# A chain of two transformer blocks on one core: the list scheduler's clock with a read port shared by VectorE and GpSimd, and the additions of the norms on VectorE

## The chip, the cores and the metric

The kernel runs on one core of one Trainium2 chip. The metric is the device time of one execution in microseconds (us); the median of three runs before the change is 2174.5 us (2173.39 to 2176.55). Engines are called PE (TensorE, matrix multiplication), DVE (VectorE), ACT (ScalarE), POOL (GpSimd) and SP (SyncE, here an issuer of DMAs).

## The reference

The input is one sequence of 512 tokens of width 1024, all in float32. Two chains of layers follow each other. Cut to its steps:

```
# first block
f = swiglu(rms_norm(h, g_ffn1_pre), gate, up, down);  h = h + 0.5 * rms_norm(f, g_ffn1_post)
u = rms_norm(h, g_mix_pre);  qkv = u @ w_in           # 8 heads of each of two attentions
o_a = stick_breaking_attention(...);  o_b = chunk_band_attention(...)
h = h + rms_norm(concat(rms_norm(o_a), rms_norm(o_b)) @ w_out, g_mix_post)
f = swiglu(rms_norm(h, g_ffn2_pre), ...);             h = h + 0.5 * rms_norm(f, g_ffn2_post)
e = (p @ w_ple_proj) * sigmoid(h @ w_ple_gate);       h = h + rms_norm(e, g_ple_post)
# second block, each: x = x + mixer(rms_norm_2(x, norm_w[i]))
conv_mixer      # gated causal convolution, 3 taps
fox_mixer       # softmax attention with a forget gate, 8 heads of 128
gdn_mixer       # gated delta rule in chunks, 8 heads of 128
swa_mixer       # sliding window attention with sinks, rotary positions
return rms_norm_2(x, final_norm_w)
```

rms_norm(x, g) is x * rsqrt(mean(x*x) + eps) * g over the 1024 channels of a token.

## The kernel before

**Layout.** Activations lie transposed: channels on the 128 partitions, the 512 tokens along the free axis, so the residual stream is eight tiles h[0..7] of 128x512. Weights come from HBM in chunks of 128x512 through four staging tiles wst. Each chunk, and each activation that enters a matrix multiplication, is split into a rounded high part (ACT copies to fp32r) and a remainder (DVE subtracts), and every product is three matmuls: high by high, low by high, high by low (`gemm`, `gemm_two`, `vproj`).

**Norms.** A norm is a sum over channels. `Norm.add` squares a tile on ACT and adds the square to an accumulator; the first tile is written straight to it. With `later` the addition is made on POOL (`G1`), else on DVE. `Norm.stats` turns the accumulator into means with matmuls that are one column wide (`L682`, ps<-cst,t 128x1) and takes the inverse root, on DVE and ACT with `soon`, else by 13 small operations of which 12 are on POOL (`rsqrt`). `Norm.rows` spreads the result over the partitions by transposes (`L687`). There are two kinds of joints between layers:

- `post_norm` (after ffn1, the mixing, ffn2 and the gated projection): the output f is normed and added to h, in two halves of 256 tokens. For each half and each of eight tiles: t = f * gain * r (DVE, one input in PSUM), h = h + t (POOL for the five tiles of `ON_POOL`, DVE for three), the high part (ACT), the square (ACT), its addition (POOL, where another norm follows, which is so at three of the four), and the remainder (DVE).
- `residual_gemm` (after conv, fox and gdn): each output tile is added to h from PSUM (DVE), split, squared, and the square is added on POOL, in 128x512.

**What sets the order.** The program is written out by a list scheduler that runs while the kernel is traced. `Eng.__getattr__` gives each operation of ACT, DVE, POOL and SP a cost in ns and queues it as an `Op`; `free` holds the time at which each engine is free, `at` and `used` when each part of a tile was written and last used, `LAG` the delay from one engine to another. `next_op` picks the operation that can start first, and among those within 20 ns of it the one of lowest priority number (`V0` and `A0` have -1, `V`, `A` and `G` 0, `V1`, `A1` and `G1` 1; weight splits -2 where they are needed soon, else 1). PE is written by the main sequence of matmuls; after each product `poll` lets tasks (attention heads, norms) take a turn when their inputs were ready 150 ns before PE's clock (`MARGIN`). `thin` keeps short matmuls from following each other for long. `mm` and `transpose` price PE's instructions. Each engine then works through its instructions in the order written; semaphores keep the data right, so a price that is wrong makes an engine wait, and nothing else.

```
AHEAD = 300.0
MARGIN = 150.0
POOL = {"affine_select": (127, 0.91), "memset": (36, 0.83), "tensor_scalar": (160, 1.0), "tensor_copy": (120, 3.3)}
```

Nearly all operations of ACT, DVE, POOL and SP are issued at one line of a helper, L391, so rows are told apart by tiles: h is the residual stream, wst a weight chunk, ps a PSUM bank, t any 128x512 work tile, b and a small ones.

Of the kernel before, what the change touches and what calls it, by code (L numbers as in the profile page):

```python
# [12 lines left out]
ALU = mybir.AluOpType  # L13
# [188 lines left out]
def chain_kernel(ctx, tc, xT, pT, wall, params, consts, chbias, pos, out):  # L202
# [83 lines left out]

    class Op:


        def __init__(self, key, run, outs, ins, cost, prio=0, func=None, more=0):  # L290
            self.key, self.run, self.outs, self.ins, self.cost, self.more = key, run, outs, ins, cost, more
            self.prio, self.func = prio, func
            self.deps, self.next = set(), []
            for x, w in [(x, True) for x in outs] + [(x, False) for x in ins]:
                for o in conflicts(x, w):
                    if o not in self.deps:
                        self.deps.add(o)
                        o.next.append(self)
            for x, w in [(x, True) for x in outs] + [(x, False) for x in ins]:
                live.setdefault(name(x), []).append((self, parts(x)[0], w))  # L300
            pending[key].append(self)
# [10 lines left out]
        def start(self):  # L312
            return max([free[self.key]] + [there(x, self.key) for x in self.ins] + [unused(x, self.key) for x in self.outs])

        def trace(self):
            for o in list(self.deps):
                o.trace()
            t = self.start() + self.cost
            k = self.load()
            if k is not None:  # L320
                table[0] = k
                t += 1280
            self.run()
            free[self.key] = t
            pending[self.key].remove(self)
            for x in self.outs + self.ins:
                live[name(x)] = [e for e in live[name(x)] if e[0] is not self]
            key, t = (self.key, t) if not self.more else ("SP", t + self.more)
            for x in self.ins:
                touch(x, t, key)  # L330
            for x in self.outs:
                touch(x, t, key, True)
            for o in self.next:
                o.deps.discard(self)

    def next_op():

        best, when = None, NEVER
        for ops in pending.values():
            can = [(o.start(), o) for o in ops if not o.deps]  # L340
            if can:
                t0 = min(c[0] for c in can)
                t, o = min((c for c in can if c[0] <= t0 + 20), key=lambda c: c[1].rank())
                if t < when:
                    best, when = o, t
        return best, when
# [11 lines left out]
    class Eng:  # L358
# [6 lines left out]
        def __getattr__(self, op):  # L365
            f = getattr(self.eng, op)

            def call(*a, **kw):
# [22 lines left out]
                Op(self.key, lambda: f(*a, **kw), outs, ins, cost, self.prio, func, more)  # L391
# [276 lines left out]

    def mm(ps, lhsT, rhs, start=True, stop=True, tile=None, **kw):
        ps, lhsT, rhs = raw(ps), raw(lhsT), raw(rhs)  # L670
        n = max(parts(rhs)[1], 64)
        if tile is not None:
            ns = tile
        elif rhs.dtype == F32:
            ns = 4 * n / 2.4 + 2.5
        elif rhs.dtype == F32R:
            ns = (n if n >= 256 else 4 * n) / 2.4 + 2.5
        else:
            ns = n / 2.4
        thin[0] = max(0.0, thin[0] + (ns if tile is not None else -0.5 * ns))  # L680
        product(ps, (lhsT, rhs), ns)
        PE.matmul(ps, lhsT, rhs, start=start, stop=stop, **kw)  # L682

    def transpose(ps, src, idn):
        ps, src, idn = raw(ps), raw(src), raw(idn)
        product(ps, (src, idn), 107.0)
        PE.transpose(ps, src, idn)  # L687
# [110 lines left out]
    class Norm:  # L798
# [8 lines left out]
        def add(self, src, cols, later=False):  # L807
# [7 lines left out]
            else:  # L815
                sq = T("sq")
                a.activation(sq[:, c], src, AF.Square)
                (G1 if later else V0).tensor_tensor(self.acc[:, c], self.acc[:, c], sq[:, c], ALU.add)

        def stats(self, cols, soon=False):  # L820
# [3 lines left out]
            for j in range(c0 // P, c1 // P):  # L824
                mm(pc[:, j : j + 1], self.acc[:, j * P : j * P + P], meanc[:, self.mcol : self.mcol + 1], start=j == c0 // P,
                   skip_group_check=True, tile=187)
# [82 lines left out]
    def post_norm(pn, f, gain, nxt_gain, with_norm):  # L909
# [3 lines left out]
        def go(cols):  # L913
            c = slice(*cols)

            def g():
# [5 lines left out]
                for k in range(9):  # L922
                    if k < 8:
                        t = T("pt")
                        V.scalar_tensor_tensor(t[:, c], f[k][:, c], gain[:, k : k + 1], rb, ALU.mult, ALU.mult)
                        (G if k in ON_POOL else V).tensor_tensor(h[k][:, c], h[k][:, c], t[:, c], ALU.add)
# [173 lines left out]
    def soft_heads(heads, span, done, own, causal=False, ready=lambda: True):  # L1100
# [46 lines left out]
        def weigh(qt):  # L1147
            k0, n = span(qt)
            for j in range(n // P):
                for i, (rows, qk, bias, values, sinks) in enumerate(heads):  # L1150
                    mm(po[rows, qt * P : qt * P + P], values(k0 // P + j), ptb[qt, i][:, j * P : j * P + P],
                       start=j == 0, stop=j == n // P - 1, skip_group_check=True, tile=134 if len(heads) > 1 else None)
# [24 lines left out]
    def mixing(S1):  # L1177
# [45 lines left out]
        def sb_pair(p):  # L1223
# [93 lines left out]
            for kt in range(4):  # L1317
                for e in range(2):
                    hd = 2 * p + e
                    mm(po[rows[e], kt * P :], va[kt][:, hd * 64 : hd * 64 + 64], at_(a[place[kt, e][0]], kt, e), start=kt == 0, stop=kt == 3, skip_group_check=True,  # L1320
                       tile=0.95 * (S - kt * P))
# [285 lines left out]
    def gdn_layer(S1):  # L1607
# [18 lines left out]
        def gates(t):  # L1626
            yield t[0:64]
            pt = PS("bat")
            for c in range(4):
                mm(pt[:, c * 16 : c * 16 + 16], t[0:64, c * P : c * P + P], con("ident32")[0:64, 0:16], tile=187)  # L1630
# [60 lines left out]
        def head(hd):  # L1691
# [88 lines left out]
            def mm32(ps, lhsT, rhs):  # L1780
                for c in range(4):
                    for g in range(4):
                        gs, cs = slice(32 * g, 32 * g + 32), slice(32 * c, 32 * c + 32)
                        mm(ps[gs, cs], lhsT[gs, cs], rhs[gs, cs], tile=34)
# [27 lines left out]
            for c in range(4):  # L1812
                cs = slice(32 * c, 32 * c + 32)
                for a, b in zip(lo, hi):
                    mm(p5[b, cs], nL[a, c * P + b.start : c * P + b.stop], Tm[a, cs], tile=34)
# [8 lines left out]
            for c in range(4):  # L1824
                cs = slice(32 * c, 32 * c + 32)
                mm(p7[hi[0], cs], U[hi[0], cs], M5[hi[0], cs], tile=34)
                for a, b in zip(lo, hi):
                    mm(p6[a, cs], M5[b, cs], U[b, cs], tile=34)
# [6 lines left out]
            for c in range(4):  # L1835
                cs = slice(64 * c, 64 * c + 64)
                mm(p8[64:P, cs], nL[0:64, c * P + 64 : c * P + P], T64[0:64, cs], tile=50)
# [302 lines left out]
```

## Time and profile before

| what | value |
|---|---|
| median of three runs | 2174.5 us |
| profiled execution, its own time | 2176.79 us |
| its span, first to last instruction | 2175.1 us |
| PE busy | 2116.3 us, 97% |
| DVE, ACT, POOL busy | 1324.4, 999.2, 299.5 us |
| mean granted clock of PE | 0.99 |

The own time of the profiled execution is 1.7 us more than its span. Times in rows are us from the span's start unless they say ns. In a timeline row the first number is the start, the second the length, xN how many instructions are merged, and the bracket holds the idle time before and what ended it. Consecutive instructions of one engine overlap a little, so a group's busy time can be more than the stretch it fills.

### The profile page before, as it was taken

What the parts mean: (1) busy time and instruction counts of PE and PEld (TensorE: products, weight loads), DVE (VectorE), ACT (ScalarE), POOL (GpSimd) and SP (SyncE); (2) the same over time, 40 slices, a digit from 0 to 9 for tenths busy, and PEclk for the clock granted to TensorE, in tenths of its full rate; (3) what the DMA queues carried; (4) which work ended last, traced back from release to release, by engine and by line L of the source; (5) the groups of instructions that cost most, each with busy time, mean ns of one, the idle gap of its engine ahead of it and who ended that gap; (6) DMA issues with size and microseconds to landing.
All of it is one profiled execution on the core that took longest, in us unless ns stands there. A gap on an engine that the chain in (4) does not pass through costs nothing.

```text
span 2175.1 us, 35809 instructions
## 1 busy us (share of the span) xinstructions
PE 2116.3 (97%) x13583; PEld 1778.1 (82%) x13583; DVE 1324.4 (61%) x2783; ACT 999.2 (46%) x2187; POOL 299.5 (14%) x600
## 2 busy tenths in 40 slices
PE   8999999999999999999999999999998999999998
PEld 7888889988779888889988887888877877778777
DVE  5433455787867442455785554266568677665896
ACT  5332333676855332333642234344446554533764
POOL 0000001311113000000120012000015242221320
PEclk9999999999999999999999999999999999999999
DMA  5232241222221332232223333312222222222221
GB/s 170 97 97 93 96 139 56 69 70 81 64 88 52 105 112 83 97 115 71 92 73 97 97 97 115 116 59 68 69 85 70 60 55 59 61 83 86 85 83 59
DMA packets 105404, 186.11 MB, mean 86 GB/s; under 512 B 12392, under 2 KB 18952, under 8 KB 105232
## 3 DMA queue, kind: packets, MB, share of 16 engines
q1 hardware_dynamic: 103920, 179.62, 26.6%
q0 software_dynamic: 1312, 4.21, 0.6%
q8 instruction: 106, 1.74, 0.3%
q14 instruction: 66, 0.54, 0.1%
HBM read 179.03 MB, written 2.13 MB: 83 GB/s over the span
## 4 chain that ended last, share of the span: by engine, by line
PE 82%; DVE 11%; POOL 3%; ACT 2%; issue 2%; DMA 1%; SPq 0%; DVEq 0%; POOLq 0%; ACTq 0%
PE ps L682 80%; DVE t L391 9%; ACT t L391 2%; PE ps L687 2%; POOL b L391 2%; DVE h L391 1%; POOL t L391 1%; DVE b L391 0%; DMA wst<-in_wall_dram 0%; DMA h<-in_xT_dram 0%; ACT L391 0%; DVE pad L391 0%; SPq L391 0%; POOL h L391 0%; DVE a L391 0%
## 5 line engine op out<-in xcount | busy, mean ns | idle before, releaser
L682 PE MATMUL ps<-t,t 128*128 128x512 f32 (+4 forms) x10648 | 2035.2, 353 | 22.1 <-ACT t L391 11.3
L682 PEld LDWEIGHTS ps<-t,t 128*128 128x128 f32 (+2 forms) x10648 | 1678.2, 186 | 320.7 <-issue 24.4
L391 DVE TENSOR_TENSOR t<-wst,t 128x512 fp32r<-128x512 f32 (+1 forms) x646 | 448.4, 719 | 252.6 <-ACT t L391 250.7
L391 ACT ACTIVATE t<-t 128x512 f32<-128x512 f32 (+4 forms) x470 | 260.3, 569 | 608.8 <-DVE t L391 602.0
L391 ACT ACTIVATE t<-wst 128x512 fp32r<-128x512 f32 (+1 forms) x646 | 380.8, 621 | 98.3 <-DMA wst<-in_wall_dram 94.9
L391 DVE TENSOR_TENSOR t<-ps,t 128x512 f32<-128x512 f32 (+2 forms) x247 | 156.1, 638 | 297.7 <-PE ps L682 296.0
L391 DVE TENSOR_TENSOR t<-t,t 128x512 fp32r<-128x512 f32 (+6 forms) x387 | 238.4, 631 | 66.7 <-ACT t L391 60.8
L391 ACT ACTIVATE t<-ps 128x512 f32<-128x512 f32 (+5 forms) x357 | 140.5, 418 | 239.0 <-PE ps L682 155.5
L391 POOL TENSOR_TENSOR t<-t,t 128x512 f32<-128x512 f32 (+1 forms) x99 | 120.0, 1213 | 542.1 <-ACT t L391 463.7
L391 POOL TENSOR_TENSOR h<-h,t 128x256 f32<-128x256 f32 x40 | 34.7, 874 | 795.5 <-DVE t L391 793.9
L391 ACT ACTIVATE t<-t,a 128x257 f32<-128x257 f32 (+5 forms) x128 | 66.2, 518 | 49.4 <-DVE a L391 46.8
L391 ACT ACTIVATE t<-h,prm 128x256 fp32r<-128x256 f32 (+1 forms) x80 | 46.4, 588 | 83.4 <-DVE h L391 69.8
L391 DVE SCALAR_TENSOR_TENSOR t<-h,prm,t 128x256 fp32r<-128x256 f32 (+1 forms) x80 | 64.2, 815 | 9.0 <-ACT t L391 9.0
L391 DVE SCALAR_TENSOR_TENSOR t<-pad,prm,t 128x512 f32<-128x512 f32 (+1 forms) x92 | 68.7, 755 | 0.8
L687 PE MATMUL ps<-cst,t 128*128 128x128 f32 x400 | 63.1, 279 | 2.5 <-DVE t L391 1.7
L391 ACT ACT_TABLE_LOAD x48 | 61.6, 1283 | 5.7 <-DVE a L391 4.1
L687 PEld LDWEIGHTS ps<-cst,t 128*128 128x128 f32 x400 | 48.6, 143 | 14.8 <-DVE t L391 2.5
L391 ACT ACTIVATE t<-h 128x256 f32<-128x256 f32 (+2 forms) x112 | 49.6, 466 | 22.6 <-DVE h L391 20.3
L391 POOL TENSOR_SCALAR b<-b 128x4 f32<-128x4 f32 (+3 forms) x84 | 26.1, 310 | 206.8 <-DVE b L391 201.7
L682 PEld LDWEIGHTS ps<-t 32*32 32x32 f32 (+1 forms) x2304 | 33.1, 109 | 24.3 <-DVE t L391 10.4
L391 DVE TENSOR_SCALAR t<-t,a 128x256 f32<-128x256 f32 (+3 forms) x128 | 49.2, 394 | 2.3
L391 POOL TENSOR_SCALAR_AFFINE_SELECT t<-t 128x256 f32<-128x256 f32 (+2 forms) x48 | 27.3, 571 | 168.0 <-DVE t L391 117.1
(93 smaller groups left out, 693.1 us busy)
## 6 DMA issues: line engine op xcount, KB each, us to landing
wst<-in_wall_dram SPq DMA_DIRECT2D x644, 256.0 KB, 2.7
t<-t SPq DMA_DIRECT2D x40, 64.0 KB, 2.0
h<-in_xT_dram SPq DMA_DIRECT2D x8, 256.0 KB, 5.3
t<-in_chbias_dram POOLq DMA_DIRECT2D x8, 256.0 KB, 3.7
t<-cdr POOLq DMA_DIRECT2D x8, 256.0 KB, 6.4
t<-gdr SPq DMA_DIRECT2D x32, 64.0 KB, 3.7
out_dram<-t SPq DMA_DIRECT2D x16, 128.0 KB, 1.8
cst<-in_consts_dram SPq DMA_DIRECT2D x1, 626.0 KB, 6.3
```

The costliest lines, as they stand in the source:

```text
L391: Op(self.key, lambda: f(*a, **kw), outs, ins, cost, self.prio, func, more)
L682: PE.matmul(ps, lhsT, rhs, start=start, stop=stop, **kw)
L687: PE.transpose(ps, src, idn)
```

## The change

A DVE operation that reads two wide operands from SBUF, or is one of tensor_scalar, tensor_copy and memset without a PSUM input, and every POOL operation that is no DMA, is marked `shared`; in the scheduler's clock such operations start one after another (`port`). Operations on 32 to 127 partitions cost 115 ns more. Prices of PE's instructions are altered, with 95 ns more where the tile mode changes (`changed`). The additions of `post_norm` to h and those of `Norm.add` with `later` go to DVE. `ON_POOL` is used nowhere else.

```diff
+    port = [0.0]
...
-        def __init__(self, key, run, outs, ins, cost, prio=0, func=None, more=0):
+        def __init__(self, key, run, outs, ins, cost, prio=0, func=None, more=0, shared=False):
             self.key, self.run, self.outs, self.ins, self.cost, self.more = key, run, outs, ins, cost, more
+            self.shared = shared
...
-        def start(self):
-            return max([free[self.key]] + [there(x, self.key) for x in self.ins] + [unused(x, self.key) for x in self.outs])
+        def start(self, port_too=True):
+            t = max([free[self.key]] + [there(x, self.key) for x in self.ins] + [unused(x, self.key) for x in self.outs])
+            return max(t, port[0]) if self.shared and port_too else t
...
             free[self.key] = t
+            if self.shared:
+                port[0] = t
...
-        best, when = None, NEVER
+        best, when = None, (NEVER, NEVER)
...
                 t, o = min((c for c in can if c[0] <= t0 + 20), key=lambda c: c[1].rank())
+
+                t = t, o.start(False)
                 if t < when:
                     best, when = o, t
-        return best, when
+        return best, when[0]
...
-                Op(self.key, lambda: f(*a, **kw), outs, ins, cost, self.prio, func, more)
+                if op != "dma_start" and any(32 <= x.ap[0][1] < P for x in outs + ins):
+                    cost += 115
+                wide = [x for x in ins if parts(x)[1] > 1]
+                shared = self.key == "POOL" or self.key == "DVE" and not ps and (len(wide) > 1 or op in self.FAST)
+                Op(self.key, lambda: f(*a, **kw), outs, ins, cost, self.prio, func, more, shared and op != "dma_start")
...
+    mode = [(P, P)]
+    CHANGE = 95.0
+
+    def changed(rows, cols):
+        new = tuple(next(x for x in (32, 64, P) if n <= x) for n in (rows, cols))
+        if new == mode[0]:
+            return 0.0
+        mode[0] = new
+        return CHANGE
...
-        n = max(parts(rhs)[1], 64)
+        n = parts(rhs)[1]
         if tile is not None:
             ns = tile
         elif rhs.dtype == F32:
-            ns = 4 * n / 2.4 + 2.5
+
+            ns = 2 * max(110.0, (2 * n + 8) / 2.4)
         elif rhs.dtype == F32R:
-            ns = (n if n >= 256 else 4 * n) / 2.4 + 2.5
+            ns = ((n if n >= 256 else 4 * n) + 32) / 2.4
         else:
-            ns = n / 2.4
+            ns = max(n, P) / 2.4 + 2.5
+        ns += changed(rhs.ap[0][1], parts(lhsT)[1])
...
-        product(ps, (src, idn), 107.0)
+        product(ps, (src, idn), 110.0 + changed(P, P))
...
-                (G1 if later else V0).tensor_tensor(self.acc[:, c], self.acc[:, c], sq[:, c], ALU.add)
+                (V1 if later else V0).tensor_tensor(self.acc[:, c], self.acc[:, c], sq[:, c], ALU.add)
...
-                        (G if k in ON_POOL else V).tensor_tensor(h[k][:, c], h[k][:, c], t[:, c], ALU.add)
+                        V.tensor_tensor(h[k][:, c], h[k][:, c], t[:, c], ALU.add)
...
-                   skip_group_check=True, tile=187)
+                   skip_group_check=True, tile=220)
...
-                        mm(ps[gs, cs], lhsT[gs, cs], rhs[gs, cs], tile=34)
+                        mm(ps[gs, cs], lhsT[gs, cs], rhs[gs, cs], tile=25)
```

Seven more fixed prices of small matmuls change in the same way (`tile=` 134 to 110, 0.95 to 0.84 of a length, 187 to 220, three times 34 to 40, 50 to 124).

## Rows read from the trace of the kernel before

**Rows 1.** The page, busy time of each engine over the whole span.
```profile
PE 2116.3 (97%) x13583; PEld 1778.1 (82%) x13583; DVE 1324.4 (61%) x2783; ACT 999.2 (46%) x2187; POOL 299.5 (14%) x600
```
**Rows 2.** Waits of PE: us in total, times, longest us.
```profile
PE ps L682 <- DVE t L391: 22.9, 25, 2.7
PE ps L682 <- ACT t L391: 11.6, 9, 5.4
PE ps L682 <- POOL t L391: 6.0, 3, 2.9
...
PE ps L687 <- POOL b L391: 3.9, 2, 2.7
```
**Rows 3.** Stretches: length, PE, PEld, DVE, ACT, POOL busy, granted clock, DMA share, GB/s.
```profile
350.00:400.00 50.00, 46.03 (x376) 44.84 (x375) 39.41 (x91) 21.74 (x54) 22.57 (x27) 1.00 0.20 59
...
570.00:655.00 85.00, 75.82 (x409) 60.18 (x408) 59.71 (x130) 59.06 (x123) 15.65 (x40) 0.90 0.22 71
655.00:700.00 45.00, 41.97 (x344) 40.98 (x344) 35.71 (x85) 26.54 (x63) 21.53 (x24) 1.00 0.17 49
...
1020.00:1125.00 105.00, 98.98 (x808) 97.97 (x808) 84.77 (x201) 61.40 (x135) 28.91 (x36) 0.98 0.22 69
...
1640.00:1700.00 60.00, 54.39 (x770) 41.63 (x769) 47.31 (x106) 31.44 (x101) 28.06 (x59) 0.94 0.29 80
...
1930.00:1975.00 45.00, 39.37 (x165) 31.77 (x164) 35.05 (x52) 18.04 (x32) 16.71 (x20) 0.92 0.18 54
```
**Rows 4.** Groups by form: busy us, mean ns of one, idle before. GpSimd's additions.
```profile
L391 POOL TENSOR_TENSOR t<-t,t 128x512 f32<-128x512 f32 x57 | 82.5, 1449 | 526.1 <-ACT t L391 448.8 <-DMA t<-t 46.7 <-DVE a L391 19.0
...
L391 POOL TENSOR_TENSOR t<-t,t 128x256 f32<-128x256 f32 x42 | 37.5, 894 | 16.0 <-ACT t L391 14.9
...
L391 POOL TENSOR_TENSOR h<-h,t 128x256 f32<-128x256 f32 x40 | 34.7, 874 | 795.5 <-DVE t L391 793.9 <-ACT t L391 0.8 <-DVE b L391 0.8
```
**Rows 5.** Groups by form from 361.1 to 398.1, first joint: VectorE, then GpSimd.
```profile
L391 DVE SCALAR_TENSOR_TENSOR t<-h,prm,t 128x256 fp32r<-128x256 f32 x16 | 11.9, 746 | 0.0
L391 DVE TENSOR_TENSOR t<-wst,t 128x512 fp32r<-128x512 f32 x11 | 10.3, 936 | 0.0
L391 DVE SCALAR_TENSOR_TENSOR t<-t,b,ps 128x256 f32<-128x256 f32 x16 | 7.1, 472 | 2.0 <-PE ps L687 2.0
L391 DVE TENSOR_TENSOR h<-h,t 128x256 f32<-128x256 f32 x6 | 3.0, 505 | 0.0
...
L391 POOL TENSOR_TENSOR t<-t,t 128x256 f32<-128x256 f32 x14 | 12.5, 896 | 2.9 <-ACT t L391 2.5
L391 POOL TENSOR_TENSOR h<-h,t 128x256 f32<-128x256 f32 x10 | 8.8, 890 | 371.5 <-DVE t L391 371.5
```
**Rows 6.** VectorE's groups from 100 to 300, where GpSimd is idle.
```profile
L391 DVE TENSOR_TENSOR t<-wst,t 128x512 fp32r<-128x512 f32 x74 | 47.7, 688 | 60.2 <-ACT t L391 60.2
```
**Rows 7.** VectorE's groups from 1022.2 to 1048, the joint without squares.
```profile
L391 DVE TENSOR_TENSOR h<-h,t 128x256 f32<-128x256 f32 x6 | 2.5, 416 | 0.0
```
**Rows 8.** Timeline of the fourth joint: VectorE's spacing in 128x256.
```profile
1108.75 1.07 DVE L391 TENSOR_TENSOR t<-ps,t 128x256 f32<-128x256 f32 x3
```
**Rows 9.** Timeline: PE at the joints after fox and after gdn.
```profile
1587.48 1.05 PE L682 MATMUL ps<-cst,t 128*128 128x1 f32 x8 [2.07 <-POOL t L391]
...
1952.56 1.05 PE L682 MATMUL ps<-cst,t 128*128 128x1 f32 x8 [2.89 <-POOL t L391]
...
1962.84 0.65 PE L687 MATMUL ps<-cst,b 128*128 128x128 f32 x4 [2.74 <-POOL b L391]
```
**Rows 10.** Timeline in gdn: the same four copies twice, and PE behind the second.
```profile
1663.78 0.90 DVE L391 COPY t<-t 32x128 f32<-32x128 f32 x4
...
1678.16 2.79 DVE L391 COPY t<-t 32x128 f32<-32x128 f32 x4
...
1683.38 0.45 PE L682 MATMUL ps<-t 32*32 32x32 f32 x32 [2.73 <-DVE t L391]
```
**Rows 11.** Timeline: PE in a stretch of 128x256 matmuls.
```profile
1049.75 10.46 PE L682 MATMUL ps<-t,t 128*128 128x256 f32 x85 [0.75 <-ACT t L391]
```

More of the change, by code (lines that the diff above doesn't have):

```diff
@@ L1151, in weigh @@
                     mm(po[rows, qt * P : qt * P + P], values(k0 // P + j), ptb[qt, i][:, j * P : j * P + P],
-                       start=j == 0, stop=j == n // P - 1, skip_group_check=True, tile=134 if len(heads) > 1 else None)
+                       start=j == 0, stop=j == n // P - 1, skip_group_check=True, tile=110 if len(heads) > 1 else None)
             for i in range(len(heads)):
@@ L1320, in sb_pair @@
                     mm(po[rows[e], kt * P :], va[kt][:, hd * 64 : hd * 64 + 64], at_(a[place[kt, e][0]], kt, e), start=kt == 0, stop=kt == 3, skip_group_check=True,
-                       tile=0.95 * (S - kt * P))
+                       tile=0.84 * (S - kt * P))
             a.clear()
@@ L1629, in gates @@
             for c in range(4):
-                mm(pt[:, c * 16 : c * 16 + 16], t[0:64, c * P : c * P + P], con("ident32")[0:64, 0:16], tile=187)
+                mm(pt[:, c * 16 : c * 16 + 16], t[0:64, c * P : c * P + P], con("ident32")[0:64, 0:16], tile=220)
             del t
@@ L1814, in head @@
                 for a, b in zip(lo, hi):
-                    mm(p5[b, cs], nL[a, c * P + b.start : c * P + b.stop], Tm[a, cs], tile=34)
+                    mm(p5[b, cs], nL[a, c * P + b.start : c * P + b.stop], Tm[a, cs], tile=40)
             for i, b in enumerate(hi):
@@ L1825, in head @@
                 cs = slice(32 * c, 32 * c + 32)
-                mm(p7[hi[0], cs], U[hi[0], cs], M5[hi[0], cs], tile=34)
+                mm(p7[hi[0], cs], U[hi[0], cs], M5[hi[0], cs], tile=40)
                 for a, b in zip(lo, hi):
-                    mm(p6[a, cs], M5[b, cs], U[b, cs], tile=34)
+                    mm(p6[a, cs], M5[b, cs], U[b, cs], tile=40)
             V.tensor_copy(blocks(T64[:, 0:256])[hi[0], :, 0:32], blocks(p7[:, 0:P])[hi[0]])
@@ L1836, in head @@
                 cs = slice(64 * c, 64 * c + 64)
-                mm(p8[64:P, cs], nL[0:64, c * P + 64 : c * P + P], T64[0:64, cs], tile=50)
+                mm(p8[64:P, cs], nL[0:64, c * P + 64 : c * P + P], T64[0:64, cs], tile=124)
             M6 = T64
```

## The prediction

> **What bounds the kernel now.** First the page's busy times [rows 1]: PE is busy 2116.3 of 2175.1 us, so all that a new order can win lies in the 58.8 us in which PE does nothing, and in what PE loses by its clock. DVE at 61% and POOL at 14% bound nothing over the whole; they can matter only where PE stands. So the second view is PE's waits [rows 2]: 22.9 us for DVE, 11.6 for ACT, and 6.0 + 3.9 = 9.9 for POOL, in some forty short pieces of which the longest two or three are under 3 us except one of 5.4. Third, the stretches in which the waits sit [rows 3]; the reader should subtract PE's busy time from the length of each. The joints with post_norm lose 50.00 - 46.03 = 4.0, 45.00 - 41.97 = 3.0 and 105.00 - 98.98 = 6.0 us (the last row holds two joints), 13.0 in all. The end of the mixing loses 85.00 - 75.82 = 9.2, one early part of gdn 60.00 - 54.39 = 5.6, and the joint from gdn to swa 45.00 - 39.37 = 5.6. In the last three the granted clock is below 1.00 as well: 0.90, 0.94 and 0.92 on the mean, that is, PE ran part of the time at 1.2 instead of 2.4 GHz after it had stood. Counted as the missing share of the stretch that is 0.10 x 85 = 8.5, 0.06 x 60 = 3.6 and 0.08 x 45 = 3.6 us.
>
> **The additions that leave POOL.** Three rows hold them [rows 4]: 40 additions to h, 42 of squares in 128x256, and 3 x 7 = 21 of the 57 in 128x512; the other 36 belong to gdn and swa and stay. POOL's price is 874, 894 and 1449 ns. POOL's work falls by 34.7 + 37.5 + 21 x 1.449 = 102.6 us.
>
> At the joints with post_norm the question is whether DVE has room, and the trace of the first one answers it [rows 5]: in the 37.0 us from 361.1 to 398.1 DVE is idle 2.0 us in the rows shown, so DVE paces that joint. But part of its time is not work. The remainder of h (t<-h,prm,t) takes 746 ns there, the same operation with one operand in PSUM 472; the weight remainder 936, against 688 where POOL rests [rows 6]; the addition to h 505, against 416 [rows 7]. POOL's 24 additions in that stretch thus cost DVE 16 x 0.274 + 11 x 0.248 + 6 x 0.089 = 4.4 + 2.7 + 0.5 = 7.6 us. The change gives those back and adds the 24 additions. Three operations of that size fill 1.07 us with 0.416 for the last, so one follows the other every (1.07 - 0.416) / 2 = 0.33 us [rows 8], and 24 of them are 7.9 us. The balance is +0.3 us of DVE per joint, at three joints; the one without squares gets 10 x 0.33 = 3.3 us, has less to be freed from, and has only ten of POOL's additions to lose. I take nothing for all four joints: the squares have the lower priority and slip behind the remainders that PE wants next, and the sum is level. The bounds are wide. Below, all 13.0 us of waits at these joints go. Above, DVE gets nothing back, and the 40 additions to h, which stand ahead of PE's next operand, lengthen the joints by 40 x 0.33 = 13.2 us.
>
> The Trainium skill says under "SBUF: two separate sides" of "SBUF — State Buffer" that DVE with two SBUF inputs and GpSimd take the shared ports in turn, for a whole instruction, and that the loser is blocked fully. By that, POOL's two groups [rows 5] would take their full 12.5 + 8.8 = 21.3 us from DVE, and the joint would come out 21.3 - 7.9 = 13.4 us of DVE shorter; the rows show a third of that, 7.6, since a third of DVE's operations read PSUM and POOL itself often waits. I go by the rows.
>
> At the joints with residual_gemm, DVE has room for 7 x 0.69 = 4.8 us each, since POOL no longer stretches its neighbours. PE waits there in three places [rows 9]: 2.07 and 2.89 us for the last square's addition, 2.74 for the small operations of the inverse root that follow it. A last addition on DVE takes 0.69 instead of 1.45 us, which shortens the chain by 0.76 twice, 1.5 us. Bounds: the whole 7.7 us of the three waits; or, since the addition has priority 1 and may be written behind two operations of 0.69, nothing and 2 x (1.38 - 0.76) = 1.2 us more. I take -1.5. The inverse root stays on POOL; its wait is a matter of the clock below.
>
> **The corrected clock.** It adds no instruction. Its worth is that PE is sent to a task when the task's inputs are really there, instead of standing in front of it while other matmuls are ready. So it can only return waits that the old prices caused. These are recognised by rows in which an operation took far longer than its price because POOL and DVE met. Three are those of [rows 9]: the main sequence of the next layer still has matmuls to give, and PE stands all the same. Another is in gdn [rows 10]: four copies of 32x128 take 0.90 us once and 2.79 us later, beside POOL, and PE then waits 2.73 us for what is behind them; there is a second wait like it in that stretch, which loses 5.6 us in all [rows 3]. Joints and gdn together are 7.7 - 1.5 + 5.6 = 11.8 us; I take two thirds, -7.9, as the wait can be filled only where matmuls are left. With the waits goes part of the time at the lower clock, 3.6 + 3.6 = 7.2 us in the two stretches; at the same two thirds -4.8. Bounds: all of it, -19.0; or, where the new prices send PE to a task too late and the chains of the heads grow, as much the other way as the shortest third of it, +6.
>
> PE's own prices: a 128x256 matmul took 10.46 / 85 = 0.123 us [rows 11], the old price is 256 / 2.4 + 2.5 = 109 ns, the new (256 + 32) / 2.4 = 120. In the joints, which work in halves, the old clock believed PE faster than it is and so left slack by mistake; with the new one this slack is gone, but no wait follows as long as the other prices hold. I take 0 and keep 0 to +3 as its bound.
>
> The end of the mixing, the second stretch of [rows 3], is full on DVE and ACT with little POOL (15.65 of 85 us); no addition of the change is there. A new order moves it by chance: 0, with -8 to +8 of the 17.7 us that it loses in waits and clock.
>
> Moved instructions issue no DMA. POOL's queue also carries the bias loads and the broadcasts of fox: they come sooner if anything, since POOL is freer. SP's queue sees the weight loads in the order of the plan as before, with times that shift by a few us; four staging tiles and chunks loaded several ahead hide this. No wait is added but for the V1 additions, behind which DVE's weight remainders stand for 0.33 or 0.6 us; the chunks are loaded 3 to 11 ahead of their use.
>
> **The sum.** -1.5 + 0 - 7.9 - 4.8 + 0 = -14.2 us. The profiled execution has a span of 2175.1 us and an own time of 2176.79, 1.7 more; its successor would have 2161 and 2162.8. The median of the runs is 2.3 us below the profiled one, so the time is 2174.5 - 14.2 = 2160.3 us.
>
> **Rivals.** *The waits only move* (no change): PE is already 97% busy, each wait that is filled takes a matmul from a later one, and the joint still ends when its last remainder is there. For it: the joints' balance of DVE is level (+0.3), and waits for DVE and ACT are 34.5 of the 58.8 us, which no change of POOL touches. Against it: three waits are plainly POOL's. Only the 1.5 us and some chance are left: 2172, between 2170 and 2178.
>
> *DVE is too full at the joints* (slower): the place is the second half of each post_norm, where PE takes each remainder as it comes. If DVE's stretched rows do not shorten, since they are stretched by something other than POOL, the 13.2 us of additions to h come on top, and a corrected clock earns only half of its 12.7 us: 13.2 - 6.3 = +7, 2181.5. It decides if t<-h,prm,t stays above about 0.6 us at the first joint, half way between 472 and 746. For it, DVE idles 2.0 of 37.0 us there; against it, the weight remainder falls to 688 ns where POOL rests.
>
> *The joints open* (much faster): with POOL out of the port, DVE's stretched rows and the chain through POOL vanish together and the 13.0 us of waits at the four joints go too: -27, 2147.5. For it: each h that went through POOL took 0.87 us and two hand-overs. Against it: DVE's sum is level. The rule quoted above from the page "SBUF — State Buffer" of the Trainium skill, taken fully, leads here too.
>
> **How the numbers follow.** Forecast 0.51, only moved 0.18, DVE too full 0.20, joints open 0.11. The measurement tells a change from none at about 0.2%, 4.3 us. The forecast's own range is 2152 to 2168, all of it faster; with the last rival that is 0.62. The first rival is within the bound: 0.18. The second is slower: 0.20. The range takes in the first rival, the lower part of the second and nearly all of the last: 2146 to 2180.
>
> **What would show it.** PE's waits for POOL t fall from 6.0 to under 1 us; POOL is busy near 197 us; DVE's t<-h,prm,t at the first joint is near 0.47 us; DVE is busy some 20 to 30 us more over the whole, since 82 x 0.42 + 21 x 0.69 = 49 us of additions come and the stretching goes; the stretch after gdn loses under 3 us and its clock is near 1.00; the four joints lose about as much as before. I am wrong if the joints lose over 20 us, or if the mixing's end or gdn, where nothing was moved, shifts by more than 10 us.

## The result, and the profile after

The changed kernel takes 2150.65 us (median of 4 runs, 2149.27 to 2151.62) against 2175.28 us before (4 runs, 2173.39 to 2176.55): a ratio of 0.9887 [0.9870, 0.9904], 24.6 us less, where 14.2 were forecast: inside the range of 2146 to 2180, and 1.4 us below the forecast's own range of 2152 to 2168. The profiled execution has an own time of 2149.27 us, a span of 2147.6 and a mean granted clock of 0.994 (before: 0.990).

The page after, busy time of each engine, as in [rows 1]:

```profile
PE 2104.5 (98%) x13583; PEld 1772.0 (83%) x13583; DVE 1315.1 (61%) x2886; ACT 1004.8 (47%) x2189; POOL 193.6 (9%) x497
```

PE stands 2147.6 - 2104.5 = 43.1 us instead of 58.8, and is busy 11.8 us less for the same 13583 matmuls. 103 instructions went from POOL to DVE, yet DVE is busy 9.3 us less.

PE's waits after, as in [rows 2] (us in total, times, longest us; L404, L708 and L713 are the lines that were L391, L682 and L687):

```profile
PE ps L708 <- ACT t L404: 15.6, 10, 5.3
PE ps L708 <- DVE t L404: 10.2, 14, 2.2
PE ps L713 <- DVE b L404: 5.4, 4, 1.8
...
PE ps L708 <- POOL b L404: 0.5, 1, 0.5
```

The waits for POOL t are gone, those for POOL b fell from 3.9 to 0.5. But the largest fall is in the waits for DVE t, from 22.9 to 10.2, and 8.6 of these 12.7 us lie in the gdn layer (9.7 before, 1.1 after), where only the 7 squares of its last joint were moved. Before, in that layer (1584.0 to 1949.1):

```profile
PE ps L682 <- DVE t L391: 9.7, 10, 2.7
PE ps L682 <- POOL t L391: 2.1, 1, 2.1
```

The stretches after, as in [rows 3], moved with the work that they hold; the last row is the whole gdn layer, from the start of the last write of h in fox to that of the last in gdn:

```profile
350.00:400.00 50.00, 49.51 (x412) 48.99 (x411) 38.95 (x112) 21.55 (x54) 1.88 (x5) 1.00 0.22 69
570.00:655.00 85.00, 71.33 (x391) 57.61 (x390) 57.72 (x130) 54.82 (x115) 12.36 (x42) 0.92 0.25 78
650.00:700.00 50.00, 46.59 (x373) 45.88 (x372) 38.33 (x113) 27.11 (x64) 0.00 (x0) 0.97 0.15 43
1015.00:1125.00 110.00, 104.98 (x851) 103.54 (x850) 88.07 (x242) 63.51 (x138) 0.00 (x0) 0.98 0.22 68
1640.00:1700.00 60.00, 59.85 (x967) 45.19 (x966) 53.55 (x124) 32.26 (x84) 22.24 (x42) 1.00 0.30 87
1907.00:1952.00 45.00, 45.00 (x220) 37.95 (x219) 36.11 (x63) 19.56 (x34) 7.01 (x13) 1.00 0.21 62
1578.00:1925.60 347.60, 344.78 (x4027) 276.31 (x4026) 250.26 (x604) 186.87 (x532) 103.95 (x285) 1.00 0.24 69
```

The same layer before:

```profile
1584.00:1949.10 365.10, 352.10 (x4034) 281.71 (x4033) 255.59 (x601) 183.31 (x530) 112.85 (x292) 0.99 0.23 67
```

PE stood 365.1 - 352.1 = 13.0 us in gdn before and stands 2.8 now; the layer is 17.5 us shorter. The first joint is nearly closed (0.5 us lost instead of 4.0), the others are as they were, and the end of the mixing loses more in this stretch (13.7 instead of 9.2).

VectorE's groups at the first joint after, from 360.4 to 399, as in [rows 5]:

```profile
L404 DVE SCALAR_TENSOR_TENSOR t<-h,prm,t 128x256 fp32r<-128x256 f32 x16 | 7.6, 478 | 0.0
L404 DVE TENSOR_TENSOR t<-wst,t 128x512 fp32r<-128x512 f32 x11 | 7.5, 683 | 0.0
...
L404 DVE TENSOR_TENSOR h<-h,t 128x256 f32<-128x256 f32 x16 | 6.6, 417 | 0.0
```

746 ns became 478, 936 became 683, 505 became 417. These are the undisturbed durations: 472 for the like operation with one input in PSUM [rows 5], 688 and 416 [rows 6, 7]. With POOL's additions gone the stretching is gone, so POOL was what stretched them.

A table by segments shows where the time moved. Landmarks are the first one-column matmul of the norm after ffn1, the mixing, ffn2 and the gated projection (ple), and the last write of h in conv, fox, gdn and swa (us, from the traces; the kernels are explained below):

| kernel | start | mixing | ffn2 | ple | conv | fox | gdn | swa |
|---|---|---|---|---|---|---|---|---|
| before | 358.5 | 298.7 | 362.4 | 53.6 | 238.5 | 272.3 | 365.1 | 215.4 |
| after | 357.8 | 295.1 | 363.9 | 54.9 | 236.6 | 269.7 | 347.6 | 211.1 |
| moves_only | 359.4 | 303.7 | 365.0 | 53.5 | 247.0 | 269.6 | 359.9 | 212.0 |
| prices_only | 358.2 | 306.9 | 365.7 | 56.3 | 240.3 | 272.9 | 368.3 | 215.9 |
| clock_only | 357.9 | 294.6 | 362.5 | 53.2 | 233.9 | 270.6 | 348.3 | 210.2 |
| moves_prices | 357.4 | 300.2 | 364.3 | 56.4 | 243.2 | 269.8 | 361.0 | 216.4 |
| port_no_pe_prices | 358.1 | 309.4 | 360.2 | 52.9 | 235.7 | 269.7 | 344.2 | 217.6 |
| port_in_gdn_only | 357.3 | 299.9 | 364.2 | 56.4 | 243.0 | 269.8 | 347.5 | 216.3 |
| h_on_gpsimd | 357.6 | 294.4 | 359.3 | 53.3 | 243.6 | 269.6 | 347.7 | 211.1 |
| squares_on_gpsimd | 357.6 | 294.4 | 359.7 | 54.9 | 233.7 | 270.6 | 348.1 | 210.0 |

### The profile page after: what moved, and what is told of

Read it like the earlier page. It is cut to its first block, busy times and chain, and to the rows that moved or that the text cites. A ratio compares the mean times of both kernels' runs of the same rounds, so it can differ in the third digit from the quotient of the medians.

```text
span 2147.6 us, 35751 instructions
## 1 busy us (share of the span) xinstructions
PE 2104.5 (98%) x13583; PEld 1772.0 (83%) x13583; DVE 1315.1 (61%) x2886; ACT 1004.8 (47%) x2189; POOL 193.6 (9%) x497
## 4 chain that ended last, share of the span: by engine, by line
PE 89%; DVE 6%; ACT 3%; issue 1%; DMA 1%; POOL 0%; SPq 0%; DVEq 0%; ACTq 0%; POOLq 0%
PE ps L708 87%; DVE t L404 5%; ACT t L404 2%; PE ps L713 2%; DVE h L404 1%; ACT L404 0%; DVE b L404 0%; DMA wst<-in_wall_dram 0%; POOL b L404 0%; DMA h<-in_xT_dram 0%; SPq L404 0%; POOL t L404 0%; DVE a L404 0%; ACT b L404 0%; DVE pad L404 0%
## 5 line engine op out<-in xcount | busy, mean ns | idle before, releaser
L708 PE MATMUL ps<-t,t 128*128 128x512 f32 (+4 forms) x10648 | 2025.7, 352 | 23.8 <-ACT t L404 15.6
L708 PEld LDWEIGHTS ps<-t,t 128*128 128x128 f32 (+1 forms) x10648 | 1674.0, 186 | 318.1 <-issue 22.0
L404 DVE TENSOR_TENSOR t<-wst,t 128x512 fp32r<-128x512 f32 (+1 forms) x646 | 434.2, 697 | 261.5 <-ACT t L404 260.0
L404 ACT ACTIVATE t<-t 128x512 f32<-128x512 f32 (+4 forms) x470 | 260.6, 572 | 571.2 <-DVE t L404 562.1
L404 ACT ACTIVATE t<-wst 128x512 fp32r<-128x512 f32 (+1 forms) x646 | 382.2, 622 | 108.2 <-DMA wst<-in_wall_dram 105.2
L404 DVE TENSOR_TENSOR t<-ps,t 128x512 f32<-128x512 f32 (+2 forms) x247 | 156.3, 638 | 262.1 <-PE ps L708 257.8
L404 DVE TENSOR_TENSOR t<-t,t 128x512 fp32r<-128x512 f32 (+5 forms) x450 | 266.8, 606 | 73.7 <-ACT t L404 67.1
L404 ACT ACTIVATE t<-ps 128x512 f32<-128x512 f32 (+5 forms) x357 | 140.3, 420 | 229.2 <-PE ps L708 151.7
L404 POOL TENSOR_SCALAR b<-b 128x4 f32<-128x4 f32 (+3 forms) x84 | 22.6, 270 | 1127.5 <-DVE b L404 1122.7
L404 ACT ACTIVATE t<-t,a 128x257 f32<-128x257 f32 (+5 forms) x128 | 66.4, 520 | 42.4 <-DVE a L404 39.3
L404 ACT ACTIVATE t<-h,prm 128x256 fp32r<-128x256 f32 (+1 forms) x80 | 45.9, 589 | 70.6 <-DVE h L404 68.9
L404 ACT ACT_TABLE_LOAD x50 | 64.2, 1283 | 13.2 <-DVE a L404 6.7
L404 DVE SCALAR_TENSOR_TENSOR t<-pad,prm,t 128x512 f32<-128x512 f32 (+1 forms) x92 | 66.4, 730 | 1.2
L713 PE MATMUL ps<-cst,t 128*128 128x128 f32 x400 | 62.0, 275 | 2.6 <-DVE t L404 1.4
L404 ACT ACTIVATE t<-h 128x256 f32<-128x256 f32 (+2 forms) x112 | 49.5, 467 | 23.3 <-DVE h L404 23.3
L713 PEld LDWEIGHTS ps<-cst,t 128*128 128x128 f32 x400 | 46.9, 140 | 12.5 <-DVE t L404 3.6
L404 POOL TENSOR_TENSOR t<-t,t 128x512 f32<-128x512 f32 x36 | 50.0, 1391 | 73.8 <-DMA t<-t 48.1
L404 DVE SCALAR_TENSOR_TENSOR t<-h,prm,t 128x256 fp32r<-128x256 f32 (+1 forms) x80 | 46.0, 585 | 7.7 <-ACT t L404 7.6
L708 PEld LDWEIGHTS ps<-t 32*32 32x32 f32 (+1 forms) x2304 | 32.5, 109 | 20.0 <-issue 6.3
L404 DVE TENSOR_SCALAR t<-t,a 128x256 f32<-128x256 f32 (+3 forms) x128 | 47.5, 382 | 1.7
L404 DVE CUSTOM_DVE_ANT_0 t<-ps,t 128x128 f32<-128x128 f32 (+3 forms) x64 | 30.5, 487 | 26.2 <-PE ps L708 25.2
L404 DVE COPY t<-ps 128x128 f32<-128x128 f32 (+3 forms) x73 | 25.0, 344 | 32.3 <-PE ps L708 31.5
```

## Experiments

The kernel before was run beside each group on the same chip: 2175.57 us (14 runs) for moves_only, clock_only, prices_only and moves_prices; 2176.46 (13) for port_no_pe_prices, h_on_gpsimd, squares_on_gpsimd and before_margin_130; 2176.29 (7) for the other four.

**The two halves of the change, and the port apart from the prices.** *moves_only* is the kernel before with the additions on VectorE and the old clock:

```diff
-                (G1 if later else V0).tensor_tensor(self.acc[:, c], self.acc[:, c], sq[:, c], ALU.add)
+                (V1 if later else V0).tensor_tensor(self.acc[:, c], self.acc[:, c], sq[:, c], ALU.add)
...
-                        (G if k in ON_POOL else V).tensor_tensor(h[k][:, c], h[k][:, c], t[:, c], ALU.add)
+                        V.tensor_tensor(h[k][:, c], h[k][:, c], t[:, c], ALU.add)
```

> Only the additions are moved to VectorE, with the old clock. Theory 'clock' (most of the gain is the scheduler's new clock, the moved additions are level by themselves): between 2170 and 2178 us. Rival 'moves' (GpSimd in the shared port was the trouble, and taking its 103 us of additions away gives the gain in any order): 2155 or less, with PE's waits behind the gdn layer gone. Rival 'chance' (every new order moves the time by some 10 us either way): anywhere between 2160 and 2190.

Measured: 2184.1 us (2182.54 to 2184.77), 1.0036 [1.0023, 1.0050]. The moves alone cost 8.5 us. Both theories missed; only the wide band of 'chance' holds it.

*clock_only* is the changed kernel with these two lines as before:

```diff
-                (V1 if later else V0).tensor_tensor(self.acc[:, c], self.acc[:, c], sq[:, c], ALU.add)
+                (G1 if later else V0).tensor_tensor(self.acc[:, c], self.acc[:, c], sq[:, c], ALU.add)
...
-                        V.tensor_tensor(h[k][:, c], h[k][:, c], t[:, c], ALU.add)
+                        (G if k in ON_POOL else V).tensor_tensor(h[k][:, c], h[k][:, c], t[:, c], ALU.add)
```

> All of the new clock, port and prices, with the additions left on GpSimd. Theory 'clock': at least two thirds of the 24.6 us, 2159 or less, and PE's waits for GpSimd at the joints after fox and gdn under 2 us together instead of 7.7. Theory 'moves': 2170 or more. 'Both needed': between, about 2163.

Measured: 2143.14 us (2142.55 to 2143.74), 0.9849 [0.9834, 0.9864]. The scheduler's new clock alone gains 32.4 us, more than the whole change: theory 'clock', and PE's waits for POOL are down to 0.7 us in the whole kernel.

*prices_only* is clock_only without the port; *moves_prices* is the changed kernel without it:

```diff
-                Op(self.key, lambda: f(*a, **kw), outs, ins, cost, self.prio, func, more, shared and op != "dma_start")
+                Op(self.key, lambda: f(*a, **kw), outs, ins, cost, self.prio, func, more, False)
```

> The additions stay on GpSimd and nothing is marked as sharing the port; only PE's prices, the price of a changed tile mode and the 115 ns for narrow operations are new. Theory 'clock' with the port as its working part: 2170 to 2178, no change. Rival 'prices' (PE's prices, 109 against a measured 123 ns for 256 columns, are what misled the scheduler): 2160 or less. Theory 'moves': no change.

Measured: 2197.16 us (2196.14 to 2198.69), 1.0098 [1.0083, 1.0113]. No theory had a loss of 21.6 us.

> The changed kernel without the port in its clock: moves and prices. If the port is what works, the gdn layer gets its waits back and the time is 2165 or more. If moves with prices are enough, because most of the operations that collided are no longer on GpSimd, 2153 or less.

Measured: 2180.69 us (2177.38 to 2182.62), 1.0022 [1.0012, 1.0031], as the theory that the port is what works had it.

| us | additions on GpSimd | additions on VectorE |
|---|---|---|
| old clock | 2175.6 | 2184.1 |
| new prices, no port | 2197.2 | 2180.7 |
| new prices and port | 2143.1 | 2150.7 |

The port is worth 54.0 us in the first column and 30.0 in the second; the prices without it cost 21.6 us in the first and gain 3.4 in the second. The moves help (16.5 us) only where the scheduler's clock is otherwise new and does not know the port; where it does, they cost 7.5 us.

Does the port gain because the engines collide less? VectorE's groups of clock_only at the first joint, 360.4 to 399:

```profile
L404 DVE TENSOR_TENSOR t<-wst,t 128x512 fp32r<-128x512 f32 x11 | 9.6, 879 | 0.0
L404 DVE SCALAR_TENSOR_TENSOR t<-h,prm,t 128x256 fp32r<-128x256 f32 x16 | 9.1, 593 | 0.3 <-ACT t L404 0.3
```

They are stretched less than before (936 and 746), but still by 196 and 115 ns a piece against the changed kernel, and this kernel is 7.5 us faster than the one where they are not. The pages of prices_only and clock_only, the same instructions without and with the port in the scheduler's clock:

```profile
PE 2120.9 (97%) x13583; PEld 1782.5 (81%) x13583; DVE 1320.5 (60%) x2783; ACT 1009.0 (46%) x2191; POOL 297.5 (14%) x600
PE 2101.8 (98%) x13583; PEld 1770.3 (83%) x13583; DVE 1304.4 (61%) x2783; ACT 1004.1 (47%) x2189; POOL 291.1 (14%) x600
```

So where GpSimd keeps its additions the engines do collide less, by 16.1 us of VectorE's busy time. Where it has given them up they hardly collide less: VectorE is busy 1317.2 us in moves_prices and 1315.1 in the changed kernel, and the port is still worth 30.0 us. There, what helps is that the order allows for the lengthening. How the 54.0 us of the first column divide between the two is not shown.

**The prices of PE.** *port_no_pe_prices* is clock_only with all prices of PE's instructions as before (and no charge for a changed tile mode):

```diff
-            ns = ((n if n >= 256 else 4 * n) + 32) / 2.4
+            ns = (n if n >= 256 else 4 * n) / 2.4 + 2.5
...
-        ns += changed(rhs.ap[0][1], parts(lhsT)[1])
...
-                        mm(ps[gs, cs], lhsT[gs, cs], rhs[gs, cs], tile=25)
+                        mm(ps[gs, cs], lhsT[gs, cs], rhs[gs, cs], tile=34)
```

> The additions stay on GpSimd, the port is in the clock with the 115 ns for narrow operations, PE's prices and the tile change are the old ones. After the first four runs the theory is: the port alone makes the gain, and the prices matter only with it. Theory 'port alone': within 5 us of 2143 (clock only). Rival 'port and prices together': 2160 or more. 'Chance': no telling, 2140 to 2195.

Measured: 2159.84 us (2159.42 to 2161.88), 0.9926 [0.9911, 0.9941]. Theory 'port alone' missed. With the port, PE's new prices are worth 2159.8 - 2143.1 = 16.7 us. They are earned in the mixing (309.4 against 294.6) and swa (217.6 against 210.2); gdn is short without them (344.2, with them 348.3). So gdn owes its gain to the port, here with the 115 ns.

**The port in one layer.** *port_in_gdn_only* is the changed kernel with the port known only while the gdn layer is written:

```diff
+    only = [False]
...
-                Op(self.key, lambda: f(*a, **kw), outs, ins, cost, self.prio, func, more, shared and op != "dma_start")
+                Op(self.key, lambda: f(*a, **kw), outs, ins, cost, self.prio, func, more, shared and only[0] and op != "dma_start")
...
+    only[0] = True
     st = gdn_layer(st)
+    only[0] = False
```

> The changed kernel with the port in the clock only while the gdn layer is written; elsewhere it is as in the run with moves and prices (2180.7 us, whose gdn layer, from the last addition to h of fox to that of gdn, is 361.0 us, against 347.6 in the changed kernel). Theory 'the port works where the two engines meet': the gdn layer falls to 345 to 352, the layers before it stay within 2 us, and the time is 2164 to 2172. Rival 'the gain of gdn comes from the state in which it is entered': gdn stays above 356 and the time above 2174.

Measured: 2166.87 us (2164.25 to 2167.50), 0.9953 [0.9938, 0.9967]: 13.8 us less than moves_prices. gdn takes 347.5 instead of 361.0 us, every other segment is within 0.4 us of moves_prices. This is what the theory had. Nearly half of the port's 30.0 us is thus shown to be in gdn; by the table the rest is in conv (6.6), swa (5.3) and the mixing (5.1). The layer in moves_prices, as a stretch:

```profile
1591.30:1952.40 361.10, 348.78 (x4027) 279.01 (x4026) 252.38 (x605) 189.52 (x534) 100.56 (x285) 1.00 0.23 67
```

PE's waits in it, in moves_prices:

```profile
PE ps L708 <- DVE t L404: 9.7, 10, 4.0
PE ps L713 <- DVE t L404: 1.5, 2, 0.8
```

And in the same layer of the changed kernel:

```profile
PE ps L708 <- DVE t L404: 1.1, 3, 0.4
PE ps L713 <- ACT t L404: 0.9, 1, 0.9
```

Without the port PE stands 361.1 - 348.8 = 12.3 us, with it 2.8; the waits that go are for VectorE, whose work there runs beside 285 operations of POOL in either kernel. The longest is 4.04 us. From the timeline of moves_prices, VectorE ahead of it and PE, and then the stretch behind it:

```profile
1655.49 2.50 DVE L404 COPY t<-t 32x128 f32<-32x128 f32 x4
1661.02 0.45 PE L708 MATMUL ps<-t 32*32 32x32 f32 x32 [4.04 <-DVE t L404]
1660.00:1670.00 10.00, 8.98 (x125) 6.87 (x125) 9.69 (x27) 5.48 (x14) 2.27 (x4) 0.83 0.28 81
```

Four copies take 2.50 us there beside POOL's work, where four like them took 0.90 in [rows 10]; a wait for VectorE can thus be in part POOL's doing. The other 4.0 us of the layer are PE's busy time, 348.78 against 344.78. The stretches read 1.00 for the granted clock in both, but behind the long wait it is 0.83 for 10 us, 1.7 us by its missing share; why the same matmuls take the remaining 2.3 us less is not settled.

**Which of the moved additions cost.** *h_on_gpsimd* is the changed kernel with the additions to h back on POOL (the second pair of lines in the diff of clock_only), *squares_on_gpsimd* the one with the 63 additions of squares back on it (the first pair).

> The changed kernel with the 40 additions to h back on GpSimd; the squares' additions stay on VectorE. Moving everything cost 7.5 us against the new clock alone (2143.1 to 2150.7). Theory 'full VectorE at the joints' (the additions to h stand ahead of PE's next operand): most of it comes back, 2143 to 2146. Rival 'the squares' (they carry the cost): about 2150.

Measured: 2148.27 us (2146.53 to 2148.70), 0.9870 [0.9855, 0.9884]: above the theory's 2143 to 2146, and nearer to the rival.

> The changed kernel with the 63 additions of squares back on GpSimd; the additions to h stay on VectorE. The counterpart of the run before: if the additions to h carry the cost, about 2150; if the squares do, 2143 to 2146; if the cost is a chance of the order and belongs to neither, both runs may come out anywhere from 2138 to 2160.

Measured: 2141.16 us (2140.57 to 2141.54), 0.9838 [0.9824, 0.9853]. The squares on VectorE cost 2150.65 - 2141.16 = 9.5 us (with h on POOL 2148.27 - 2143.14 = 5.1), the additions to h -2.0 us with the squares on POOL or +2.4 with them on VectorE.

*squares_of_halves_on_gpsimd* puts back only the 42 squares of `post_norm`:

```diff
-        def add(self, src, cols, later=False):
+        def add(self, src, cols, later=False, on=None):
...
-                (V1 if later else V0).tensor_tensor(self.acc[:, c], self.acc[:, c], sq[:, c], ALU.add)
+                (on or (V1 if later else V0)).tensor_tensor(self.acc[:, c], self.acc[:, c], sq[:, c], ALU.add)
...
-                            S2.norm.add(h[k][:, c], cols, True)
+                            S2.norm.add(h[k][:, c], cols, True, G1)
```

> The changed kernel with the 42 additions of squares of the joints that work in halves on GpSimd, the 21 of the joints after conv, fox and gdn on VectorE. Theory 'VectorE is full in the halves': nearly all of the 9.5 us of the run with all squares on GpSimd comes back, 2141 to 2144. Rival 'the other 21': about 2150.

Measured: 2142.11 us (2140.99 to 2142.47), 0.9840 [0.9826, 0.9855]: 8.5 of the 9.5 us are the squares in halves. Where they cost is seen in the stretches that begin at the joints after the mixing and after ple. The changed kernel:

```profile
652.90:702.90 50.00, 46.59 (x372) 45.85 (x371) 39.61 (x115) 28.74 (x67) 0.00 (x0) 0.97 0.11 33
1071.70:1123.70 52.00, 48.70 (x392) 48.12 (x391) 44.63 (x129) 30.73 (x68) 0.00 (x0) 0.97 0.14 41
```

squares_on_gpsimd:

```profile
652.00:702.00 50.00, 48.69 (x391) 47.73 (x390) 39.11 (x106) 29.97 (x70) 12.51 (x14) 1.00 0.17 50
1066.60:1118.60 52.00, 50.66 (x405) 49.23 (x404) 45.02 (x122) 31.55 (x69) 11.84 (x16) 1.00 0.18 54
```

PE loses 3.4 and 3.3 us against 1.3 and 1.3, and the granted clock 0.03 of 102 us, 3.1: together 7.1 us, and the segments ffn2 and conv are 4.2 and 2.9 us shorter with the squares on POOL. The second half's sum of squares comes later when VectorE has to make it. PE's rows in the changed kernel, at the joint after the mixing and then after ple:

```profile
694.81 0.50 PE L708 MATMUL ps<-cst,t 128*128 128x1 f32 x4
696.65 0.43 PE L713 MATMUL ps<-cst,b 128*128 128x128 f32 x2 [0.88 <-DVE b L404]
1115.28 0.50 PE L708 MATMUL ps<-cst,t 128*128 128x1 f32 x4
1117.12 0.43 PE L713 MATMUL ps<-cst,b 128*128 128x128 f32 x2 [1.33 <-DVE b L404]
```

squares_on_gpsimd, the same one-column matmuls:

```profile
686.08 0.50 PE L708 MATMUL ps<-cst,t 128*128 128x1 f32 x4
1105.41 0.50 PE L708 MATMUL ps<-cst,t 128*128 128x1 f32 x4
```

Counted from the starts of the stretches they come after 41.9 and 43.6 us in the changed kernel, after 34.1 and 38.8 with the squares on POOL; PE then has too few matmuls left to fill the inverse root that follows. What happens there is plainest in moves_only, at the joint after ple; PE's rows with waits:

```profile
1113.13 1.01 PE L682 MATMUL ps<-cst,t 128*128 128x1 f32 x4 [10.17 <-DVE t L391]
1116.47 0.69 PE L687 MATMUL ps<-cst,b 128*128 128x128 f32 x2 [2.33 <-DVE b L391]
```

VectorE there, the end of its rows before PE goes on:

```profile
1111.92 0.42 DVE L391 TENSOR_TENSOR t<-t,t 128x256 f32<-128x256 f32 x1
1112.26 0.48 DVE L391 SCALAR_TENSOR_TENSOR t<-h,prm,t 128x256 fp32r<-128x256 f32 x1
1112.66 1.21 DVE L391 TENSOR_TENSOR t<-t,t 128x256 f32<-128x256 f32 x3
```

And the stretch of that wait:

```profile
1102.90:1113.10 10.20, 0.06 (x1) 0.00 (x0) 10.20 (x29) 6.26 (x16) 0.00 (x0) 0.66 0.18 52
```

PE stands 10.2 us in front of a norm's one-column matmuls until the sum of squares is complete; VectorE is busy for every one of them, with operations of `post_norm` (t<-t,b,ps, h<-h,t and t<-h,prm,t) ahead of the sum's last additions, and the granted clock falls to 0.66 (between 1.2 and 2.4 GHz on the mean). conv is 247.0 us, 8.5 more than before, as much as moves_only costs in all (the other segments, the mixing with +5.0 and gdn with -5.2 first, cancel). The same wait is in moves_prices (6.65 us) and h_on_gpsimd (6.29); in the changed kernel it is not, and its loss is the smaller one above.

**How far an order is chance.** `MARGIN` from 150 to 130 ns changes no work and no price, only when tasks are let in:

```diff
-    MARGIN = 150.0
+    MARGIN = 130.0
```

> The kernel before, with MARGIN 130 instead of 150 ns: nothing of the change, only another order. Theory 'chance is large': the time moves by 5 us or more, and differences of that size between orders say nothing by themselves. Rival 'orders of one clock are alike': within 3 us of 2175.

Measured: 2176.52 us (2174.67 to 2179.11), 1.0001 [0.9991, 1.0010]: the rival.

> The changed kernel with MARGIN 130 instead of 150 ns, another order of the same work. Theory 'the squares cost 9.5 us': within 3 us of 2150.7, as the kernel before was with the same edit. Rival 'chance of the order': 5 us or more away, and then the squares' share is not settled.

Measured: 2155.56 us (2152.47 to 2156.75), 0.9900 [0.9883, 0.9916], 4.9 us more than at 150. The theory missed, and the rival's 5 us are just not reached; conv is 243.3 us, with the wait at the joint after ple at 6.95.

The last is squares_on_gpsimd with the same line:

> The run with the squares on GpSimd (2141.2 us) with MARGIN 130. Theory 'the squares cost 9.5 us': within 3 us of 2141 and at least 5 us faster than the changed kernel with the same MARGIN. Rival 'chance': the two kernels with MARGIN 130 differ by less than 5 us.

Measured: 2139.42 us (2139.24 to 2139.57), 0.9829 [0.9814, 0.9843], 1.7 us less than at 150 and the fastest kernel of all. The squares cost 2155.56 - 2139.42 = 16.1 us in this pair. In three pairs of one edit the order alone moved the time by up to 4.9 us, so nothing is read into differences of about 5 us: the 9.5 and 16.1 us of the squares and the 30 to 54 of the port are above that, the 5.1 us of the squares beside h on POOL and the 2 us of the additions to h are not, and stay open.

## Why the prediction was right and wrong

**Right in the number, in part by luck.** The scheduler's clock gained 19.7 us more than its term and the moves cost 7.5 us where they were to gain 1.5, an error of 9.0: the two errors have opposite signs, and so the time came out only 9.7 us below the forecast.

**Right: what gains.** The corrected clock returns waits, as the step of that name said, and the forecast sign follows from it. PE's waits for POOL t are gone, POOL is busy 193.6 us (197 foreseen), and the joint from gdn to swa loses nothing at a clock of 1.00. PE's groups there:

```profile
1929.38 0.95 PE L708 MATMUL ps<-cst,t 128*128 128x1 f32 x8
1930.19 10.51 PE L708 MATMUL ps<-t,t 128*128 128x512 f32 x45
1940.54 0.60 PE L713 MATMUL ps<-cst,b 128*128 128x128 f32 x4
```

The two brackets that [rows 9] has at this joint are empty: 45 matmuls of swa run while POOL takes the inverse root, which stayed on it.

**Mis-sized: "The corrected clock", -7.9 - 4.8 = -12.7 us.** Measured: -32.4 us alone. The term counted only waits in which a row showed POOL at work: the joints after fox and gdn and one stretch of gdn with 5.6 us lost. The whole gdn layer lost 13.0, 10.2 of which went, though PE's waits there name VectorE for 10.2 us and POOL for 2.1; the wait for a VectorE operation that was late because of POOL carries VectorE's name, as the 4.04 us above do in part. The bound of -19 us had the same gap. With PE's busy time gdn has 16.8 of the 32.4 us; swa has 5.2, conv 4.6 and the mixing 4.1, whose waits were not followed one by one. One condition was named under which I would be wrong, a shift of gdn by more than 10 us: it shifted by 17.5, the right way, and this is why. (That nothing was moved in gdn is not quite so: the 7 squares of its last joint were. And the row of the third and fourth joints in [rows 3] reads 0.98 for the granted clock, some 2 us that the term did not count.) The rows of the lost time of each layer as a whole would have shown it.

**Mis-sized: PE's prices, taken as 0.** They are worth -16.7 us where the port is known and +21.6 together with the 115 ns of narrow operations where it is not. An interaction of some 38 us is not found edit by edit; how much of it belongs to the 115 ns, which were in both kernels with the port, was not tried.

**Wrong in sign: the moves, -1.5 + 0.** Measured +8.5 with the old clock, +7.5 with the new. The balance of VectorE at a joint was nearly right: the durations fell as [rows 5 to 7] said. What failed is "the squares have the lower priority and slip behind the remainders that PE wants next, and the sum is level". They do slip, and the norm's sum is then complete only when VectorE has run dry: in moves_only PE has nothing else, as in the 10.17 us above, and in the changed kernel the second half's sum is 7.8 and 4.8 us later. On POOL the squares ran beside that work and cost VectorE little: t<-h,prm,t at the three joints takes 515 ns on the mean with them there and 477 without. The Trainium skill, "GPSIMD Engine Reference", section "Engine selection", says that an elementwise addition belongs on VectorE, as GpSimd is about twice as slow with two inputs. The durations agree (0.42 against 0.89 us [rows 4]), the time of the kernel does not: 2141.2 us with the squares on the slower, idle engine, 2150.7 on the faster, full one.

**The step on VectorE's busy time**, +20 to 30 us, was wrong: -9.3 us. The groups that got the additions grew by 11.8 + 12.8 + 16.1 = 40.7 us, not 49, since the operations already in them became shorter. Against that, weight remainders fell by 14.0 us and the remainders of h by 9.7 in halves and 8.6 in whole tiles; the last, at the joints with `residual_gemm`, I had not counted. That form before took 1006 ns; in VectorE's groups after:

```profile
L404 DVE SCALAR_TENSOR_TENSOR t<-h,prm,t 128x512 fp32r<-128x512 f32 x32 | 23.0, 746 | 7.6 <-ACT t L404 7.6
```

**The rivals.** *Only moved* fell: the time in which PE stands went from 58.8 to 43.1 us. *DVE too full at the joints* has its place and a price (8.5 us beside the 13.2 foreseen) but not its cause, which is the squares and not the additions to h, nor its test: t<-h,prm,t fell to 0.48 us and the joint filled up all the same; and the clock outweighs it. *The joints open* named 2147.5 us, close to the time, for a reason that is not there: the four joints still lose 0.5 + 3.4 + 5.0 = 8.9 of their 13.0 us. The Trainium skill's rule of the exclusive lock ("SBUF — State Buffer", section "SBUF: two separate sides"), taken as fully as the prediction took it, would give back 21.3 us at the first joint; the rows gave 16 x 0.268 + 11 x 0.253 + 6 x 0.088 = 7.6, the figure of the prediction.

**Not settled:** why PE is busy 11.8 us less for the same matmuls; the granted clock, 0.990 against 0.994, accounts for some 0.004 x 2148 = 9 of them, an estimate. The port without the 115 ns of narrow operations was not tried, nor a plain surcharge on VectorE's and GpSimd's prices in its place.

## What to carry to other kernels

Where a list scheduler orders the work, first give its clock the resources that two engines share, then refine single prices: here better prices without the port lost 21.6 us (with the additions moved they gained 3.4), and with it the same prices were part of a gain of 32. Take a change of placement and a change of the model apart, in all four combinations, before believing either; the better kernel here is the new clock with the squares left on GpSimd. And read lost time by whole layers, since a collision can be booked on the engine that was hit and not on the one that hit it.

## What the runs showed of the hardware

GpSimd's small operations suffer too. At the joint after gdn in the changed kernel ten of the thirteen operations of 128x4 in its inverse root (it has 14 with 13 on GpSimd, one more than the description of the kernel says) take 0.5 to 0.65 us each, beside a VectorE that is busy nearly all the time; in the kernel before, from 1917.0 to 1919.8 us, where VectorE stands still, they take 0.19 to 0.20. One of each, after and before:

```profile
1935.57 0.65 POOL L404 TENSOR_TENSOR b<-b,b 128x4 f32<-128x4 f32 x1
1917.03 0.20 POOL L391 TENSOR_TENSOR b<-b,b 128x4 f32<-128x4 f32 x1
```

The mean of that form over the whole span of the changed kernel is 277 ns (86 operations). The thirteen take 7.0 us together; at 277 ns each they would take 3.6, so the collisions lengthen this chain by some 3.4 us, an estimate. VectorE's lengthened operations, in turn, returned to within 6 ns of their undisturbed rows (478, 683 and 417 against 472, 688 and 416), with no remainder for another cause.
